# First mixer: four of the modulation parts beside the scan, keys and queries instead of beside the attention and the output projection

## The chip, the cores and the metric

The kernel runs on one core of one Trainium2 chip. The metric is the device time of one execution in microseconds (us), lower is better. Three runs of the kernel before took 1707.82 to 1708.36 us, with a median of 1708.34 us.

## What is computed

The reference is a backbone of two layers over 256 context tokens and 256 latent tokens, 1024 channels wide. Each layer runs three mixers on one shared input projection (a state-space scan, S5; multi-head latent attention; a Hyena long convolution), projects their normed outputs back, and then sends every token through a mixture of 32 experts. What the change moves is the modulation: each layer has six vectors of 1024 channels, worked out from the condition alone, and needed at different places.

```
mod_l = jnp.split((act_l @ ada_w[i] + ada_b[i])[:, None, :], 6, axis=-1)
hl = _modulate(xl, norm1_g[i], mod_l[0], mod_l[1])
...
xl = xl + mod_l[2] * (_merge_groups(s5_l, mla_l, hy_l, mix_norm_g[i]) @ w_out[i])
fl = _modulate(xl, norm2_g[i], mod_l[3], mod_l[4]).reshape(bsz * n, d)
...
xl = xl + mod_l[5] * y[:bsz * n].reshape(bsz, n, d)
```

Parts 0 and 1 are needed first of all, part 2 at the output projection, parts 3 and 4 at the router, part 5 after the experts. `act_l` depends on the condition and on nothing that the layers compute, so any part can be worked out at any time before its use.

## The kernel before, in words

Layer by layer there is a mixer and then the experts. Tokens lie along the free dimension (512 columns, 256 of them context), channels along the partitions in eight blocks of 128. All larger tiles in SBUF are pages of 128 x 1024 fp32 out of one pool of 44 (`NPAGE`), for loaded weights as well as for intermediate results. Loads of weights go through SP's queue, 512 KB each, in the order of the program; a load is issued when a page comes free for it.

One modulation part is `ada_part(i, part)`: eight loads of 512 KB, for each two fp32 matmuls of a 32-column stationary with 512 columns (each stands as two instructions in the trace, so 32 in a part, line 166), an eviction of the PSUM bank (line 121: on ScalarE for even parts, on VectorE for odd ones), four transposes (line 175), two reductions and an addition on VectorE (lines 178 and 179), and for parts 1 and 4 one more VectorE operation (line 183). It yields after four loads, after eight, and at its end.

The order of the work is written with `weave`, which takes one step of each of its generators in turn until all of them are at their end. From that program order a planner with a modelled timeline makes the order of each engine's queue; it may let an instruction that is ready go ahead of an earlier one that is not. The order is fixed when the kernel is built.

The first mixer goes through these stages (times from the profile):

- up to 76 us: parts 0 and 1, and the first input projections;
- first weave, 76 to 113 us: rotation and drive matrices of the scan on VectorE, the chunks, the rope keys and the query latents (projections, line 788), the last of the Hyena spectrum;
- scan weave, 113 to 161 us: the scan on VectorE, the key norm, the Hyena inputs (line 788);
- third weave, 161 to 212 us: the readout matrices of the scan (VectorE, and line 618 on TensorE), the query norm, the keys and values (lines 1016 and 1028), the queries (line 1049);
- attention weave, 212 to 348 us: `attention` (line 1091 and 1097 the scores, 1123 and 1131 the transposed probabilities, 1143 the values), `hyena_end`, `s5_end`, and `ada_rest` with five modulation parts and the start of the router (lines 665, 672 and 681). In program order a head's scores come before the transposes of the head two before it. Scores, values and the statistics of a norm share three PSUM banks;
- from 348 us: the output projection (line 1373), the router, and from 434 us the experts, whose weights are streamed to the end of the layer.

Of the kernel before, what the change touches and what calls it, by code (L numbers as in the profile page):

```python
# [55 lines left out]
def weave(*gens):  # L56

    gens = [g if isinstance(g, tuple) else (g, 1) for g in gens]
    while gens:
        left = []  # L60
        for g, n in gens:
            for _ in range(n):
                if next(g, gens) is gens:
                    break
            else:
                left.append((g, n))
        gens = left


def build(tc, A, dbg=None):  # L70
# [676 lines left out]
    def mixer(i, acc):  # L747
        pl = plan[0] = PLAN[i]
# [78 lines left out]
        def s5_scan():  # L827

            T, rho = V["rot"], V["rho"]
            Sc = V["Sc"] = [page(), page()]  # L830
            for g8 in range(2):
                stage[0] = "S5s"
                gc = slice(g8 * 512, (g8 + 1) * 512)
                Dr = page()
                D_ = [Dr[:, 0:512], Dr[:, 512:1024]]
                for ri in range(2):
                    b = bank(side=True)
                    for gg in range(8):
                        gq, g = gg // 4, gg % 4
                        nc.tensor.matmul(b[:, gg * 64:gg * 64 + 64], V["T"][ri][g8 * 2 + gq][:, g * 128:(g + 1) * 128],  # L840
                                         Ug(g8 * 8 + gg), start=True, stop=True)
                    bv = b.rearrange("p (g c) -> p g c", g=8)
                    dv = D_[ri].rearrange("p (g c) -> p g c", g=8)
                    nc.gpsimd.memset(dv[:, :, 0:1], 0.0)
                    act(dv[0:64, :, 1:64], bv[0:64, :, 0:63], AF.Copy)
                    act(dv[64:128, :, 1:33], bv[64:128, :, 31::-1], AF.Copy)
                    act(dv[64:128, :, 33:64], bv[64:128, :, 63:32:-1], AF.Copy)
                yield
                stage[0] = "S5s"
                tr, ti = T[0][:, gc], T[1][:, gc]  # L850
                Gp, x = page(), page()
                G = [Gp[:, 0:512], Gp[:, 512:1024]]
                X = [x[:, 0:512], x[:, 512:1024]]
                nc.vector.tensor_mul(X[0], D_[1], ti)
                nc.vector.tensor_mul(G[0], D_[0], tr)
                nc.vector.tensor_mul(G[1], D_[1], tr)
                nc.vector.tensor_mul(X[1], D_[0], ti)
                nc.vector.tensor_add(G[0], G[0], X[0])
                nc.vector.tensor_sub(G[1], G[1], X[1])
                for ri in range(2):  # L860
                    nc.vector.tensor_tensor_scan(D_[ri], rho[:, gc], G[ri], 0.0, OP.mult, OP.add)
                yield
                stage[0] = "S5s"
                nc.vector.tensor_mul(X[0], D_[1], ti)
                nc.vector.tensor_mul(G[0], D_[0], tr)
                nc.vector.tensor_mul(X[1], D_[0], ti)
                nc.vector.tensor_mul(G[1], D_[1], tr)
                for ri, op in ((0, OP.subtract), (1, OP.add)):
                    dv = Sc[ri][:, gc].rearrange("p (g s c) -> p g s c", g=8, s=2)
                    gv = G[ri].rearrange("p (g s c) -> p g s c", g=8, s=2)  # L870
                    xv = X[ri].rearrange("p (g s c) -> p g s c", g=8, s=2)
                    nc.vector.tensor_tensor(dv[0:64, :, s0:], gv[0:64, :, s0:], xv[0:64, :, s0:], op=op)
                    nc.vector.tensor_tensor(dv[64:128, :, s0:], gv[64:128, :, s0:, ::-1], xv[64:128, :, s0:, ::-1], op=op)
                yield
# [86 lines left out]
        def hyena_inputs():  # L961

            half = halves(nq)
            hz = V["hz"] = []
            for m in range(6):
                stage[0] = "PROJ"
                b = project(7 + m, cq0)
                o = half()
                w_ = [chp[:, CP_SW + 6 * j + m:CP_SW + 6 * j + m + 1] for j in range(3)]
                act(o, b, AF.Identity, scale=w_[1], bias=chp[:, CP_SB + m:CP_SB + m + 1])  # L970
                bv = b.rearrange("p (s t) -> p s t", t=NS)
                ov = o.rearrange("p (s t) -> p s t", t=NS)
                nc.vector.scalar_tensor_tensor(ov[:, :, 1:], bv[:, :, :NS - 1], w_[0], ov[:, :, 1:], op0=OP.mult, op1=OP.add)
                nc.vector.scalar_tensor_tensor(ov[:, :, :NS - 1], bv[:, :, 1:], w_[2], ov[:, :, :NS - 1], op0=OP.mult, op1=OP.add)  # L974
                hz.append(o)
                yield
# [17 lines left out]
        def kv_norm():  # L994
            stage[0] = "QKV"
            V["kvn"] = normed(V["kv"], CP_KVG, rstd_of(V["kv"], 256))
            yield

        def q_norm():
            stage[0] = "QKV"  # L1000
            V["cqn"] = normed(V["cq"], CP_QG, rstd_of(V["cq"], 384, nq))
            yield

        def keys_values():
            stage[0] = "QKV"
            kvn = V["kvn"]
            ukv = [weights(1 + k) for k in range(2)]
            half = halves()
            kc, vt = V["kc"], V["v"] = [], []
            yield  # L1010
            for m in range(4):
                stage[0] = "QKV"
                b = bank(side=pl["kvs"] and m % 2)
                for k in range(2):
                    for n, (a_, x_) in enumerate(three(ukv[k], kvn[k])):
                        nc.tensor.matmul(b, a_[:, m * 128:(m + 1) * 128], x_, start=(k == 0 and n == 0), stop=(k == 1 and n == 2))
                for j in range(2):
                    t = half()
                    nc.scalar.copy(t[0:64], b[64 * j:64 * j + 64])
                    nc.scalar.copy(t[64:96], V["kr"])  # L1020
                    kc.append(t[0:96])
                yield
            for t in range(4):
                stage[0] = "QKV"
                b = bank(side=pl["kvs"] and t % 2)
                for k in range(2):
                    for n, (x_, a_) in enumerate(three(kvn[k], ukv[k])):
                        nc.tensor.matmul(b, x_[:, t * 128:(t + 1) * 128], a_[:, 512:1024],
                                         start=(k == 0 and n == 0), stop=(k == 1 and n == 2))
                o = half()  # L1030
                nc.scalar.copy(o, b)
                vt.append(o)
                yield
# [244 lines left out]
        def chain(*gens):  # L1278
            for g in gens:
                yield from g  # L1280

        rstd1 = None
        if i == 0:
# [14 lines left out]
            spectrum = V["spectrum"]()  # L1298
# [10 lines left out]
            first_projections(rstd1)  # L1309
            ahead(1)  # L1310
        first = dict(r=V["rotation"], d=V["drive"] if i == 0 else lambda: iter(()), c=lambda: s5_chunks(V["u"]), a=attention_inputs)
        weave(*(first[c]() for c in pl["first"]), spectrum if i == 0 else iter(()))
        ro = V["readout"]() if i == 0 else iter(())
        n, mid = pl["ro"], pl["mid"]
        tail = iter(())
        if mid in (0, 5):
            weave(s5_scan(), chain(kv_norm(), hyena_inputs()))
            weave((ro, n), chain(q_norm(), keys_values()))
        elif mid in (1, 6):
            weave(s5_scan(), chain(kv_norm(), hyena_inputs()))  # L1320
            weave((ro, n), chain(q_norm(), keys_values(), queries()))
        elif mid in (2, 7):
            weave((chain(s5_scan(), ro), n), chain(kv_norm(), hyena_inputs(), q_norm(), keys_values()))
        elif mid in (3, 8):
            weave((chain(s5_scan(), ro), n), chain(kv_norm(), q_norm(), keys_values(), hyena_inputs()))
        elif mid in (4, 9):
            weave(s5_scan(), (ro, n), chain(kv_norm(), hyena_inputs()))
            weave(q_norm(), keys_values())
        if mid in (0, 2, 3, 4):
            weave(queries())  # L1330
        elif mid > 4 and mid != 6:
            tail = queries()
        parts = [(i, 2), (i, 3), (i, 4)] + ([(1, 1), (1, 0)] if i == 0 else []) + ([(i, 5)] if pl["late"] else [])
        Y = []

        def merged(tl, n, o_, acc=None):
# [6 lines left out]
        router = Router(i)  # L1343

        def ada_rest():
            for p in parts:
                yield from ada_part(*p)
                if p == (i, 4):
                    router.start()
                    yield  # L1350
# [726 lines left out]
```

## Time and profile before

| what | value |
|---|---|
| median of three runs | 1708.34 us |
| the profiled execution | 1709.9 us |
| its span in the profile | 1708.1 us |
| TensorE busy | 1533.8 us, 90% of the span |
| VectorE busy | 888.6 us, 52% |
| ScalarE busy | 482.4 us, 28% |
| mean granted TensorE clock | 0.953 |

The span runs from the first instruction to the last; 1.8 us of the profiled execution lie outside it. Busy time of TensorE counts a matmul from its start to its modelled end, overlaps once. PEclk is the share of the full clock that TensorE was granted: 1.00 is 2.4 GHz and 0.50 is 1.2 GHz, and a value between them is a mean over the two.

### The profile page before, as it was taken

What the parts mean: (1) busy time and instruction counts of PE and PEld (TensorE: products, weight loads), DVE (VectorE), ACT (ScalarE), POOL (GpSimd) and SP (SyncE); (2) the same over time, 40 slices, a digit from 0 to 9 for tenths busy, and PEclk for the clock granted to TensorE, in tenths of its full rate; (3) what the DMA queues carried; (4) which work ended last, traced back from release to release, by engine and by line L of the source; (5) the groups of instructions that cost most, each with busy time, mean ns of one, the idle gap of its engine ahead of it and who ended that gap; (6) DMA issues with size and microseconds to landing.
All of it is one profiled execution on the core that took longest, in us unless ns stands there. A gap on an engine that the chain in (4) does not pass through costs nothing. (4 is left out here: it accounts for less than half of the span.)

```text
span 1708.1 us, 22533 instructions
## 1 busy us (share of the span) xinstructions
PE 1533.8 (90%) x8073; PEld 788.0 (46%) x8073; DVE 888.6 (52%) x2176; ACT 482.4 (28%) x931; POOL 94.7 (6%) x154
## 2 busy tenths in 40 slices
PE   5888889998999999999899597899799999999995
PEld 1676744476433333344233387547534444333322
DVE  6769565545244546864643758455524434333333
ACT  3343544342111121112122534444311111111112
POOL 0000212003000000002000000010100000000000
PEclk9998899998999999999999698998899999999998
DMA  9111244559999999999999112577799999999994
GB/s 343 64 38 62 79 181 162 218 198 351 374 392 407 409 409 409 409 408 372 373 402 409 61 62 99 205 264 267 293 359 409 409 409 409 409 409 409 409 409 184
DMA packets 143300, 510.04 MB, mean 299 GB/s; under 512 B 17995, under 2 KB 18573, under 8 KB 142929
## 3 DMA queue, kind: packets, MB, share of 16 engines
q1 hardware_dynamic: 138736, 495.21, 75.0%
q0 software_dynamic: 4160, 12.82, 2.2%
q8 instruction: 66, 1.08, 0.3%
q10 hardware_dynamic: 288, 0.52, 0.1%
q14 instruction: 50, 0.40, 0.1%
HBM read 504.85 MB, written 3.64 MB: 298 GB/s over the span
## 5 line engine op out<-in xcount | busy, mean ns | idle before, releaser
L1582 PE MATMUL MOEp<-MOEpg,MOEpg 128*64 128x512 f32 x956 | 227.4, 603 | 13.1 <-DMA MOEpg<-in_w 11.9
L1582 PE MATMUL MOEp<-MOEpg,ROUTpg 128*64 128x512 f32 x960 | 220.5, 603 | 8.2 <-DMA MOEpg<-in_w 7.9
L1718 DVE SCALAR_TENSOR_TENSOR MOEpg<-MOEpY,MOEwt,MOEpg 64x512 fp32r<-64x512 f32 x128 | 96.0, 750 | 241.5 <-ACT MOEpg L118 241.4
L1606 PE MATMUL MOEpY<-MOEpg,MOEhT 128*64 128x512 f32 x960 | 219.4, 599 | 1.8 <-DVE MOEhT L1598 1.8
L1620 DVE SCALAR_TENSOR_TENSOR zxT<-MOEpC,zmod,zxT 128x256 f32<-128x256 f32 x385 | 168.2, 479 | 8.2 <-PE MOEpC L1698 2.1
L118 ACT ACTIVATE MOEpg<-MOEpY,MOEwt 64x512 fp32r<-64x512 f32 x128 | 87.3, 682 | 276.3 <-PE MOEpY L1606 212.2
L1588 DVE TENSOR_TENSOR MOEh<-MOEh,MOEp 128x256 f32<-128x256 f32 x65 | 27.3, 420 | 241.9 <-ACT MOEh L118 241.9
L118 ACT ACTIVATE MOEh<-MOEp 128x256 f32<-128x256 f32 x65 | 24.9, 383 | 399.7 <-PE MOEp L1582 399.7
L1688 PE MATMUL MOEpC<-MOEGT,MOEpg 128*128 128x512 f32 (+1 forms) x496 | 130.0, 364 | 6.7 <-DVE zxT L1620 6.0
L1582 PEld LDWEIGHTS MOEp<-MOEpg,ROUTpg 128*64 128x64 f32 x960 | 64.2, 137 | 149.4 <-issue 103.7
L1582 PEld LDWEIGHTS MOEp<-MOEpg,MOEpg 128*64 128x64 f32 x956 | 59.4, 136 | 159.3 <-DMA MOEpg<-in_w 90.5
L1606 PEld LDWEIGHTS MOEpY<-MOEpg,MOEhT 128*64 128x64 f32 x960 | 63.5, 136 | 120.6 <-issue 93.8
L1688 PEld LDWEIGHTS MOEpC<-MOEGT,MOEpg 128*128 128x128 f32 x496 | 75.2, 189 | 61.7 <-issue 26.8
L166 PE MATMUL ADAb<-ADApg,zcact 128*32 128x512 f32 x384 | 76.1, 614 | 12.8 <-DMA ADApg<-in_adaw 12.8
L788 PE MATMUL PROJb<-INPpg,PROJpg 128*128 128x512 f32 (+1 forms) x384 | 73.8, 356 | 6.4 <-DVE PROJpg L974 5.7
L788 PEld LDWEIGHTS PROJb<-INPpg,PROJpg 128*128 128x128 f32 x384 | 63.5, 206 | 15.9 <-ACT PROJpg L118 6.7
L118 ACT ACT_TABLE_LOAD x35 | 44.9, 1283 | 15.7 <-DVE ATTst L1102 5.7
L1657 PE MATMUL MOEpG<-MOEpg,ROUTpg 128*128 128x256 f32 x240 | 44.7, 310 | 1.1 <-DVE MOEpg L1493 1.1
L1657 PEld LDWEIGHTS MOEpG<-MOEpg,ROUTpg 128*128 128x128 f32 x240 | 33.0, 194 | 24.2 <-issue 15.8
L1091 PE MATMUL ATTb<-QKVpg,QKVpg 96*128 96x512 f32 x64 | 35.4, 654 | 7.3 <-ACT ATTpg L118 7.3
L1373 PE MATMUL OUTb<-OUTpg,ATTpg 128*128 128x512 f32 (+1 forms) x192 | 41.3, 380 | 0.0
L1373 PEld LDWEIGHTS OUTb<-OUTpg,ATTpg 128*128 128x128 f32 x192 | 34.9, 214 | 5.3 <-DVE ATTpg L230 0.2
(541 smaller groups left out, 2115.2 us busy)
## 6 DMA issues: line engine op xcount, KB each, us to landing
MOEpg<-in_w SPq DMA_DIRECT2D x719, 512.0 KB
ADApg<-in_adaw SPq DMA_DIRECT2D x96, 512.0 KB
ROUTpg<-in_w SPq DMA_DIRECT2D x61, 512.0 KB
PROJpg<-in_win SPq DMA_DIRECT2D x16, 512.0 KB
ATTpg<-in_wout SPq DMA_DIRECT2D x8, 512.0 KB
OUTpg<-in_wout SPq DMA_DIRECT2D x8, 512.0 KB
QKVpg<-in_uq SPq DMA_DIRECT2D x5, 512.0 KB
MOEpg<-in_win SPq DMA_DIRECT2D x5, 512.0 KB
```

The costliest lines, as they stand in the source:

```text
L118: nc.scalar.activation(out, in_, f, **kw)
L166: nc.tensor.matmul(b[q:q + 32, :], cact[:, k, :], w[:, h * 512:(h + 1) * 512], start=(k < 2), stop=(k >= KD - 2), tile_position=(0, q))
L788: nc.tensor.matmul(b, a_[:, c], b_[k][:, c0:], start=(first and n == 0), stop=(last and n == 2))
L1091: nc.tensor.matmul(b, qc[h][:, nq - NS + qt * 128:nq - NS + (qt + 1) * 128], kc[h], start=True, stop=True)
L1373: nc.tensor.matmul(b, a_[:, c], y_, start=(n == 0 and j == 0), stop=(n == KD - 1 and j == 2))
L1582: nc.tensor.matmul(b[64 * h:64 * h + 64, :], X[:, k, :], w[:, h * 512:(h + 1) * 512], start=(k == 0), stop=(k == KD - 1), tile_position=(0 ...
L1588: nc.vector.tensor_mul(h_, h_, b[:, 256:512])
L1606: nc.tensor.matmul(b[64 * h:64 * h + 64, :], hT[:, k % 2, (k // 2) * 64:(k // 2) * 64 + 64], w[:, h * 512:(h + 1) * 512], start=(k == 0), ...
L1620: nc.vector.scalar_tensor_tensor(xT[:, k, seg(s)], b[:, s * NS - c0:(s + 1) * NS - c0], mod[:, 40 + k, s:s + 1], xT[:, k, seg(s)], op0=OP. ...
L1657: nc.tensor.matmul(b[:, kk * 256:(kk + 1) * 256], hs[t][:, k * 128:(k + 1) * 128], G[:, t].rearrange("p e c -> p (e c)"), start=(t == 0 an ...
L1688: nc.tensor.matmul(b, Y_[p][j][rows, k * 128:(k + 1) * 128], GT_[p][rows], start=(j == 0), stop=(j == 1))
L1718: nc.vector.scalar_tensor_tensor(Y[1][rows_of, h * 512:(h + 1) * 512], b[rows], wt[rows], yh.bitcast(F32), op0=OP.mult, op1=OP.subtract)
```

## The change

Of the five parts in `ada_rest` four move. Parts (0, 2) and (0, 3) become a generator `between`, which joins the first weave and also stands in the two weaves after it; a weave runs its generators to their end, so the first one takes both parts whole. Parts (0, 4) and (1, 1) join the third weave. Part (1, 0) stays beside the attention. The start of the router, which needs parts 3 and 4, came after part (0, 4) in `ada_rest` and is now its first step. The second layer's list of parts is written out and stays what it was.

```
+        between = chain(*(ada_part(*p) for p in (((0, 2), (0, 3)) if i == 0 else ())))
-        weave(*(first[c]() for c in pl["first"]), spectrum if i == 0 else iter(()))
+        weave(*(first[c]() for c in pl["first"]), spectrum if i == 0 else iter(()), between)
...
         elif mid in (1, 6):
-            weave(s5_scan(), chain(kv_norm(), hyena_inputs()))
-            weave((ro, n), chain(q_norm(), keys_values(), queries()))
+            weave(s5_scan(), chain(kv_norm(), hyena_inputs()), between)
+            weave((ro, n), chain(q_norm(), keys_values(), queries()), chain(between, ada_part(0, 4), ada_part(1, 1)))
...
-        parts = [(i, 2), (i, 3), (i, 4)] + ([(1, 1), (1, 0)] if i == 0 else []) + ([(i, 5)] if pl["late"] else [])
+        parts = [(1, 0)] if i == 0 else [(1, 2), (1, 3), (1, 4)]
...
         def ada_rest():
+            if (i, 4) not in parts:
+                router.start()
+                yield
             for p in parts:
                 yield from ada_part(*p)
                 if p == (i, 4):
```

## Rows read from the trace of the kernel before

**Rows 1.** The page: TensorE's share, and GB/s in 40 slices.
```profile
PE 1533.8 (90%) x8073; PEld 788.0 (46%) x8073; DVE 888.6 (52%) x2176; ACT 482.4 (28%) x931; POOL 94.7 (6%) x154
...
GB/s 343 64 38 62 79 181 162 218 198 351 374 392 407 409 409 409 409 408 372 373 402 409 61 62 99 205 264 267 293 359 409 409 409 409 409 409 409 409 409 184
```

**Rows 2.** Stretches: length, busy us of PE, PEld, DVE, ACT, POOL; PEclk, DMA.
```profile
46.80:76.60 29.80, 27.28 (x129) 21.98 (x129) 23.05 (x77) 9.65 (x21) 0.00 (x0) 0.89 0.14 45
76.60:113.50 36.90, 31.81 (x139) 24.47 (x138) 28.38 (x63) 14.40 (x24) 0.28 (x3) 0.92 0.10 36
113.50:161.00 47.50, 44.22 (x230) 37.88 (x229) 36.42 (x52) 19.05 (x32) 0.15 (x2) 0.96 0.23 77
161.00:186.40 25.40, 16.54 (x57) 12.60 (x55) 22.75 (x38) 11.88 (x19) 1.97 (x4) 0.72 0.01 2
186.40:211.70 25.30, 25.17 (x342) 21.43 (x341) 6.76 (x17) 10.44 (x20) 10.73 (x21) 0.94 0.45 116
211.70:301.00 89.30, 81.60 (x439) 41.54 (x438) 53.33 (x105) 42.36 (x88) 17.50 (x16) 0.96 0.50 179
301.00:348.00 47.00, 42.21 (x269) 21.26 (x267) 25.15 (x62) 19.59 (x45) 0.00 (x0) 1.00 0.61 226
```

**Rows 3.** Waits of TensorE, 46 to 213 us: us in total, times, longest.
```profile
PE QKVb L201 <- DVE QKVpg L193: 4.4, 1, 4.4
PE S5bb L459 <- DVE S5apg L440: 3.5, 2, 3.3
...
PE QKVb L1049 <- ACT QKVpg L1019: 3.2, 1, 3.2
```

**Rows 4.** Groups on TensorE, 213 to 348 us: modulation parts and router's start.
```profile
L166 PE MATMUL ADAb<-ADApg,zcact 128*32 128x512 f32 x160 | 32.1, 603 | 0.0
...
L175 PE MATMUL ADAb<-zident,ADApg 128*128 128x128 f32 x20 | 3.1, 276 | 0.8 <-ACT ADApg L121 0.8
L681 PE MATMUL ROUTb<-zident,zmod 128*128 128x128 f32 x16 | 2.3, 282 | 0.2 <-ACT ROUTpg L121 0.2
...
L665 PE MATMUL ROUTb<-ROUTpg,zmod 128*2 128x36 f32 x16 | 0.7, 197 | 0.0
L672 PE MATMUL ROUTb<-ROUTpg,zident 2*128 2x36 f32 x4 | 0.6, 279 | 0.5 <-DVE ROUTpg L666 0.5
```

**Rows 5.** A part's small VectorE work, 211 to 348 us.
```profile
L178 DVE TENSOR_REDUCE zmod<-ADAb x10: 165/165/175, 252.6 to 341.2; 128x8 f32<-128x16 f32 x10
...
L121 DVE COPY ADApg<-ADAb x2: 692/692/692, 283.3 to 328.0; 128x512 f32<-128x512 f32 x2
```

**Rows 6.** SP's queue: loads of query weights, and SP's longest wait.
```profile
156.28 30.15 SPq L114 DMA_DIRECT2D QKVpg<-in_uq  x3
...
SPq L114 <- DVE S5cpg L600: 29.0, 1, 29.0
```

**Rows 7.** PE and ACT in order: last head, values, modulation matmuls.
```profile
322.94 1.12 PE L1091 MATMUL ATTb<-QKVpg,QKVpg 96*128 96x512 f32 x2 [0.80 <-ACT ATTpg L118]
323.99 1.05 PE L166 MATMUL ADAb<-ADApg,zcact 128*32 128x512 f32 x4
...
333.52 2.80 PE L1143 MATMUL ATTb<-ATTpg,QKVpg 128*64 128x256 f32 x22
...
336.84 2.78 PE L166 MATMUL ADAb<-ADApg,zcact 128*32 128x512 f32 x24
...
329.43 0.69 ACT L118 ACTIVATE ATTpg<-ATTb,ATTst 128x512 f32<-128x512 f32 x1 [4.00 <-DVE ATTst L1102]
...
331.22 0.48 ACT L118 ACTIVATE ATTpg<-ATTb,ATTst 128x256 f32<-128x256 f32 x1
```

**Rows 8.** Short stretches: what TensorE did and which clock it was granted.
```profile
170.00:175.00 5.00, 4.43 (x14) 3.72 (x15) 2.88 (x6) 2.09 (x5) 0.37 (x1) 0.50 0.00 0
...
225.00:230.00 5.00, 4.17 (x34) 2.89 (x34) 2.56 (x5) 0.98 (x3) 0.00 (x0) 1.00 0.00 0
...
350.00:355.00 5.00, 3.47 (x11) 2.90 (x12) 3.44 (x6) 4.99 (x7) 0.00 (x0) 0.50 0.72 288
```

## The prediction, made before the run

> **What bounds the kernel now.** I read the page first: TensorE is busy for 90% of the span, VectorE for 52%, and DMA moves 372 to 409 GB/s only while the experts stream their weights; before that it has room [rows 1]. So what counts in the first mixer is TensorE's time: its idle time, and the time in which it runs at half clock. The stretches come next [rows 2]. From 76.6 to 113.5 us TensorE is idle for 36.9 - 31.8 = 5.1 us, at a mean clock of 0.92. From 161.0 to 186.4 it is idle for 25.4 - 16.5 = 8.9 us at 0.72, while VectorE is busy for 22.75 of 25.4 us: VectorE sets the pace there. From 186.4 to 211.7 TensorE has no gap (25.17 of 25.30). In the attention weave, 211.7 to 348.0, it is busy for 123.8 of 136.3 us, so that weave is close to its work. Third, the waits: the early gaps are one or two long waits each, 3.5 us of the drive transposes for VectorE, 4.4 us of the query norm for VectorE, 3.2 us of the queries for ScalarE [rows 3]. These are single holes in a chain; work that depends on nothing can lie in them. Last, SP's queue: its loads come when pages come free, and one load of a query weight waited 29.0 us for its page [rows 6].
>
> **The price of one part.** The five parts beside the attention took 32.1 us of TensorE in line 166 and 3.1 us in line 175 [rows 4], 6.4 + 0.6 = 7.0 us each. It can be less or more: 24 of a part's 32 instructions in a row took 2.78 us, which makes 3.7 + 0.6 = 4.3 us with all pages at hand; four alone, as after the arrival of one page, took 1.05 us, which makes 8.4 + 0.6 = 9.0 us [rows 7]. I take 7.0, since the pages of the moved parts come one by one too. Four parts are 28.2 us (17 to 36).
>
> **What the early stages gain in length.** `between` is run to its end by the first weave, so two parts lie there, two in the third weave, none in the scan weave.
>
> First weave: 14.1 us come in. The room is 5.1 us of idle time and what half clock costs, 31.8 x 0.08 = 2.5 us, since steady work would keep the clock up: 7.6 us. The rest, 6.5 us, pushes back what follows, because the drive products and the key norm behind it feed the scan on VectorE.
>
> Third weave: 14.1 us come in. The room up to 186.4 us is 8.9 us idle and 16.5 x 0.28 = 4.6 us of half clock, 13.5 us. So 0.6 us are over; I take half of the clock's room as not won, 2.3 us more. VectorE, which is full here, gets two parts' small work: four reductions at 0.165 us, one copy at 0.69 us [rows 5], and four tiny operations that I price like a reduction: 2.0 us. Together 4.9 us. After 186.4 us nothing could be hidden.
>
> The loads move with them: 32 of 512 KB on SP, at the full 409 GB/s 1.28 us each, 41 us over 110 us in which DMA is busy for 1 to 23% [rows 2]. They cost no time as transfers; behind them in SP's order wait the weights of the projections, which is the page question below. Two evictions go to ScalarE, busy for less than half of each stretch. Nothing goes to POOL. Early stages: +11.4 us; bounds +2 (parts at 4.3 us lie in the holes, only VectorE's 2.0 us remain) and +30 (28.2 us beside no hole, and VectorE).
>
> **What the attention weave loses.** Up to 301 us three parts go, 21.1 us, one part (1, 0) comes, 7.0 us, and the router's start comes, 0.7 + 0.6 + 2.3 = 3.6 us [rows 4]: 10.5 us less on TensorE. Scores wait on maxima, exponentials and three PSUM banks, so a part of the freed time becomes waiting; I take a third: -7.0 us (0 to -10.5).
>
> From 301 to 348 us two parts and the router's start go, and 42.2 - 14.1 - 3.6 = 24.5 us of work remain. Now the chain of a head shows. The last head's scores began at 322.94, its first exponential ended at 330.12 and its last at 331.70 [rows 7]. Less the 1.05 us of modulation in between, a bank is back after 6.1 us and the head is through after 7.7 us. Three heads are left at 301 us, with the values of one pair between them in the same banks (2.80 us [rows 7]; with the eviction I take 3.4): 6.1 + 3.4 + 6.1 + 7.7 = 23.3 us. From 331.70 to 348.0 there are 16.3 us, of which modulation is 2.78 us and two fours at 1.05 us, 4.9 us; 11.4 remain. The tail takes 34.7 instead of 47.0 us: -12.3 us; bounds -22 (bound by 24.5 us of TensorE alone) and 0 (the clock, below).
>
> Attention weave: -19.3 us. Sum: +11.4 - 19.3 = -7.9 us. What follows (output projection, router, experts, second layer) keeps its work and its order; the experts' loads start as the output projection frees pages, so they start earlier by the same time, and the shift goes through to the end. The profiled execution took 1709.9 us, so 1702.0; the median of the runs lies 1.6 us below it: **1700 us**.
>
> **The rivals.**
> *The first weave pays in full (other side).* The order of the queues is fixed when the kernel is built. If the two parts run a page at a time, ahead of the drive transposes, and the 3.5 us hole stays where it was, the first weave grows by 18.0 us. With 4.9 and -19.3 that is +3.6: 1712. It decides from a growth of 14.4 us on. For it: the transposes waited for VectorE, and the parts do not quicken VectorE. Against: idle time of TensorE just before them is what a ready part fills.
>
> *The clock falls in the tail.* With 24.5 us of work in 34.7 TensorE is busy for 71% of the tail. In 350 to 355 us it was busy for 69% and was granted 0.50, that is 1.2 GHz; in 225 to 230 us it was busy for 83% and kept 1.00, 2.4 GHz [rows 8]. If all of the tail ran at half clock, 24.5 us would become 49, and its saving is gone: +11.4 - 7.0 = +4.4, 1713; with half of it at half clock 36.8 us, a saving of some 9 us and 1703. The Trainium skill, "TensorE: Matmul & The Clock Gate", section "HAM oscillation — how this bites in real kernels", says that matmuls fed in short bursts between waits fall back to half clock and start each burst there; by that rule the thinned tail loses what was taken out of it. The trace agrees in one place and not in the other, so I keep it as a rival. The same mechanism helps early: 170 to 175 us ran at 0.50 [rows 8].
>
> *The pages.* Three loads of query weights took 30.15 us to be issued, the last after a wait of 29.0 us for a page [rows 6], some 10 us a load. 18 pages of two parts now come ahead of the last. If a part's pages are not back in time and it slips by one such step, the queries start 10 us later: +21.4 - 19.3 = +2.1, 1710. Against: a moved part gives its pages back as soon as TensorE has used them, and in the third weave TensorE is waiting. The Trainium skill, "Perfetto Trace Analysis", section "Optimization Strategy", says that gaps that return all through a stretch can mean that SBUF has no room for the next tile; here the waits of SP agree, those of TensorE name VectorE and ScalarE [rows 3].
>
> *Waits take the place of the work.* If the heads' chain sets the weave up to 301 us already (0 instead of -7.0) and the tail gives only 10, the sum is about +1: 1709, no change.
>
> *More than forecast.* Parts at 4.3 us in the holes: early +2, attention -19.3: -17, 1691.
>
> **How the numbers follow.** Within 0.2%, 3.4 us, no change can be told. Chances: forecast 0.48 (its own range 1693 to 1707, from early +7 to +15 and attention -16 to -22), more 0.09, first weave 0.15, clock 0.12, pages 0.09, waits 0.07. Faster: nearly all of the first two, a third of the clock, a little of the rest, 0.60. Slower: most of the first weave, a third each of the clock and the pages, 0.20. The same: 0.20. The range of 8 in 10 takes in the rivals above and part of the larger gain: 1688 to 1714.
>
> **What will show it.** Right: in the first weave TensorE's wait of 3.5 us for line 440 is gone, the wait of 4.4 us for line 193 is mostly gone, and the clock between 161 and 190 us is over 0.9; the first scores come some 11 us later, at 223 us; the output projection starts near 344 us instead of 352. Wrong: those waits stand beside the parts; or the tail shows 0.5 in its clock; or the queries wait for a load; or the attention weave is no shorter than 130 us.

## The result and the profile after

The change makes the kernel slower: 1722.4 us against 1708.4 us, a ratio of 1.0086 with a 95% interval of 1.0068 to 1.0103. The forecast was 1700 with a range up to 1714. Now and then an execution falls into a slower state and takes far longer (2240.3 us, one of six of e3 below); all medians here are without such runs. The profiled execution took 1722.2 us (1709.9 before), its span is 1720.0 us (1708.1), the mean granted clock 0.949 (0.953).

Five instants are the same piece of work in every kernel here and cut the first mixer into weaves: the first chunk transposes of the scan (line 806, where the first projections end), the first drive products (840), the first keys (1016), the first scores (1091) and the first output projection (1373; 1377 in the changed kernel, where lines from 1347 on stand four later).

| us | 806 | 840 | 1016 | 1091 | 1373 | first weave | scan | third weave | attention |
|---|---|---|---|---|---|---|---|---|---|
| before | 74.4 | 113.5 | 161.0 | 211.7 | 352.4 | 39.1 | 47.5 | 50.7 | 140.7 |
| after | 74.2 | 127.3 | 174.5 | 235.8 | 361.9 | 53.1 | 47.2 | 61.3 | 126.1 |

The first weave grows by 14.0 us, the third by 10.6, the attention shrinks by 14.6. The output projection starts 9.5 us later, the first expert 9.2 us (443.3 against 434.1). From there to the end it is 1276.7 us against 1274.0; in the 18 runs below that stretch took 1271 to 1280 us, whatever was edited ahead of it, so its 2.7 us lie within that spread and are not put down to the change.

The stretches of the changed kernel (length; busy us of PE, PEld, DVE, ACT, POOL; PEclk; DMA share; GB/s), to be held against [rows 2]:

```profile
76.60:127.30 50.70, 44.53 (x208) 26.25 (x208) 29.56 (x69) 14.71 (x24) 0.28 (x3) 0.93 0.46 156
127.30:174.50 47.20, 43.92 (x231) 37.66 (x230) 36.42 (x51) 19.35 (x33) 0.15 (x2) 0.96 0.21 71
174.50:199.90 25.40, 19.39 (x91) 12.17 (x89) 22.71 (x37) 9.52 (x16) 1.11 (x3) 0.80 0.68 262
199.90:235.80 35.90, 33.24 (x378) 25.84 (x379) 8.46 (x28) 13.25 (x24) 11.52 (x23) 0.95 0.42 130
235.80:322.20 86.40, 76.06 (x410) 45.51 (x409) 52.08 (x107) 42.39 (x90) 17.32 (x16) 0.92 0.18 64
322.20:361.90 39.70, 30.37 (x167) 18.43 (x165) 21.06 (x45) 20.21 (x45) 0.00 (x0) 0.92 0.44 162
```

The last stretch runs to the output projection, 4.4 us further than the last one of [rows 2]. Cut alike, the kernel before has:

```profile
301.00:352.40 51.40, 44.16 (x281) 23.13 (x280) 26.76 (x64) 23.73 (x51) 0.00 (x0) 0.97 0.64 243
```

Read length less PE's busy time. In the first weave TensorE is idle for 6.2 us, where it was 5.1 before; in the third for 6.0 + 2.7 = 8.7, where it was 8.9 + 0.1. In sum, the idle time that was to take the parts is all still there, and TensorE's busy time stands on top of it: 12.7 and 10.9 us more. Two of the waits of [rows 3] have hardly changed; the third, 3.2 us of the queries, is gone, and one of 2.7 us for the readout (line 600) has come:

```profile
PE QKVb L201 <- DVE QKVpg L193: 4.5, 1, 4.5
PE S5bb L459 <- DVE S5apg L440: 3.7, 2, 2.5
PE S5cb L618 <- DVE S5cpg L600: 2.7, 1, 2.7
```

Why the wait for line 440 did not go is seen on VectorE and ScalarE, in order of time (start, us, instruction, idle time before it and what ended it):

```profile
105.65 0.59 ACT L121 COPY ADApg<-ADAb 128x512 f32<-128x512 f32 x1 [9.92 <-PE ADAb L166]
106.13 1.06 ACT L118 ACTIVATE PROJpg<-PROJpg 128x1024 fp32r<-128x1024 f32 x1
...
107.22 1.23 DVE L230 TENSOR_TENSOR PROJpg<-PROJpg,PROJpg 128x1024 fp32r<-128x1024 f32 x1 [5.54 <-ACT PROJpg L118]
110.92 0.26 DVE L178 TENSOR_REDUCE zmod<-ADAb 128x8 f32<-128x16 f32 x2 [2.47 <-PE ADAb L175]
...
120.82 0.69 DVE L121 COPY ADApg<-ADAb 128x512 f32<-128x512 f32 x1 [4.61 <-PE ADAb L166]
121.43 0.68 DVE L435 TENSOR_TENSOR PROJpg<-S5apg,S5apg 128x512 f32<-128x512 f32 x1
```

ScalarE stands for 9.9 us at the eviction of part 2, whose last matmuls have not run; behind it in its queue is the split of a weight (line 118), behind that on VectorE the other half of the split (230), and behind that the expansion (435 to 444) for which the drive transposes wait. The weight itself isn't late: its load was issued at 92.5 us, and the one just ahead of it landed 4.5 us after its issue, so by estimate it was there at 97 us, 9 us before its split. Twice more VectorE stands at a part's own small work, 2.5 and 4.6 us, with expansion behind it that needs nothing of the part. Together 12.6 us. The Trainium skill, "Perfetto Trace Analysis", section "Tensor Engine Instruction (MATMUL, LD_WEIGHTS)", says that ScalarE and VectorE take their instructions strictly in order; the trace agrees, line 435 starts at 121.43 us, 0.6 us after the start of the copy that held it.

On TensorE the pages' matmuls of the two parts stand alone or in small groups among the projections:

```profile
87.83 1.05 PE L166 MATMUL ADAb<-ADApg,zcact 128*32 128x512 f32 x4
...
89.40 1.06 PE L166 MATMUL ADAb<-ADApg,zcact 128*32 128x512 f32 x8
...
102.44 1.05 PE L166 MATMUL ADAb<-ADApg,zcact 128*32 128x512 f32 x4
...
104.55 1.05 PE L166 MATMUL ADAb<-ADApg,zcact 128*32 128x512 f32 x4
```

Four instructions of one page take as long as eight of two pages; what that is worth is tried below. The group rows of lines 166 and 175 over the first weave, and of line 166 over the attention, where [rows 4] had 32.1 us for five parts:

```profile
L166 PE MATMUL ADAb<-ADApg,zcact 128*32 128x512 f32 x64 | 12.7, 702 | 0.0
L175 PE MATMUL ADAb<-zident,ADApg 128*128 128x128 f32 x8 | 1.3, 280 | 0.8 <-DVE ADApg L121 0.8
...
L166 PE MATMUL ADAb<-ADApg,zcact 128*32 128x512 f32 x32 | 8.4, 605 | 0.0
```

### The profile page after: what moved, and what is told of

The parts are those of the page before. It is cut to its first block, busy times and chain, and to the rows that moved or that the text cites. A ratio compares the mean times of both kernels' runs of the same rounds, so it can differ in the third digit from the quotient of the medians.

```text
span 1720.0 us, 22536 instructions
## 1 busy us (share of the span) xinstructions
PE 1538.5 (89%) x8073; PEld 790.8 (46%) x8073; DVE 885.3 (51%) x2176; ACT 481.4 (28%) x930; POOL 94.6 (5%) x154
## 3 DMA queue, kind: packets, MB, share of 16 engines
HBM read 504.85 MB, written 3.64 MB: 296 GB/s over the span
## 5 line engine op out<-in xcount | busy, mean ns | idle before, releaser
L788 PEld LDWEIGHTS PROJb<-INPpg,PROJpg 128*128 128x128 f32 x384 | 62.1, 202 | 19.0 <-ACT PROJpg L118 6.6
L1708 POOL TENSOR_TENSOR zxT<-zxT,MOEpg 128x512 f32<-128x512 f32 (+1 forms) x6 | 6.0, 1002 | 538.9 <-ACT MOEpg L118 538.9
```

The costliest lines, as they stand in the source:

```text
L788: nc.tensor.matmul(b, a_[:, c], b_[k][:, c0:], start=(first and n == 0), stop=(last and n == 2))
```

## The experiments

All were timed beside the kernel before, whose median was 1710 to 1711 us on those chips; a ratio is to it, with its 95% interval behind it. The code fences show the edits shortened; `...` marks what is left out. Lengths are the weaves of the table above.

**Halves of the change.** e1 moves only parts (0, 2) and (0, 3); e2 only (0, 4) and (1, 1).

```
e1: weave((ro, n), chain(q_norm(), keys_values(), queries()))
    parts = [(0, 4), (1, 1), (1, 0)] if i == 0 else ...
e2: between = chain(*(ada_part(*p) for p in ()))
    parts = [(0, 2), (0, 3), (1, 0)] if i == 0 else ...      (router.start() after (0, 3))
```

> Only (0, 2) and (0, 3) move, into the first weave; (0, 4), (1, 1) and (1, 0) stay beside the attention. If the two halves of the change are independent (my theory: the cost is waits inside the first weave), the drive products start at 127 us as in the whole change (113.5 before), the first scores at 225 (+13.5 to 14), the attention gives back half of 14.7, that is 7.4: about 1715. If the halves share their cost (the rival: the 32 loads and pages of all four parts crowd each other), the drive products start before 122 us and the time is below 1711.

> Only (0, 4) and (1, 1) move, into the third weave; (0, 2), (0, 3), the router's start and (1, 0) stay beside the attention. Independent halves: drive products at 113.5 as before, third weave longer by 10.7, first scores at 222, attention 7.4 shorter: about 1712. Shared cost: third weave longer by less than 6, and a time at or below 1707.

e1: 1725.9 us (1.0075, 1.0052 to 1.0097); first weave 51.5 (+12.4), third 50.6 (as before), attention 140.1 (-0.6). e2: 1728.6 us (1.0100, 1.0083 to 1.0116); first weave 38.6, third 62.1 (+11.4), attention 146.0 (+5.3). The early costs are independent, each half pays its own. The gain is not: each half was expected to give back 7.4 us beside the attention (1715 and 1712 us in all), and neither gives back anything. In e1 TensorE is busy there for 120.5 us instead of 125.8, at a mean clock of 0.93 instead of 0.97, and idle for 19.6 instead of 14.9; two parts' matmuls are gone, and waiting and a slower clock have taken their place. Why the attention of e2 is even 5.3 us longer, no run explains.

**The finish of a part later.** e3 is e1 with the eviction, transposes, reductions and additions of the two parts put into the scan weave.

```
-        between = chain(*(ada_part(*p) for p in ...))
+        between = chain(*(ada_part(*p, finish=finish) for p in ...))    # stops behind the matmuls
-            weave(s5_scan(), chain(kv_norm(), hyena_inputs()), between)
+            weave(s5_scan(), chain(kv_norm(), hyena_inputs()), chain(*(ada_finish(*f) for f in finish)))
```

> As e1, but in the first weave only the loads and the matmuls of the two parts; their evictions, transposes, reductions and additions come in program order with the scan weave. My theory (evictions and reductions stand in the in-order queues of ScalarE and VectorE ahead of the weight splits and the expansion, and wait there for late modulation matmuls, 12.6 us of VectorE's waits): drive products at 115 to 120 us, time 1706 to 1710. Rival (the projections' weights themselves come later, because 16 modulation pages come ahead of them): drive products still at 124 to 127, time 1713 to 1716. Rival (TensorE has no room for 13 us of matmuls): the same 124 to 127, and then without waits of VectorE.

1724.0 us (1.0082, 1.0063 to 1.0100), slower than either time expected, with the drive products at 121.6, between the two expectations. First weave 46.8: 4.7 us less than in e1, so the stalls at the evictions cost about that. The time is only 1.9 us under e1's: the scan weave, where the finish now is, takes 49.6 (47.3 in e1), though it is as long in e11, e12, e15 and e18, where the finish is not in it. VectorE still waits 9.1 us in one place, for the split of a weight (line 230, here 243). The rest of the growth, 7.7 us, had another cause.

```profile
DVE PROJpg L243 <- ACT PROJpg L118: 9.7, 2, 9.1
```

**No loads.** e4 is the kernel before with two more parts in the first weave that read the resident input; e18 the same in the third weave.

```
+    spare parts: w = xT[:, k, :] in place of load(adaw[i, part, k]); result into mods[1], written again later
e4:  weave(*(first[c]() for c in pl["first"]), spectrum ..., between)
e18: weave((ro, n), chain(q_norm(), keys_values(), queries()), chain(two spare parts))
```

> The kernel before, with two more parts in the first weave that load nothing: their matmuls read the resident input instead of modulation weights, their result goes to a place that is written again later. All five real parts stay beside the attention, so the time shows the growth of the first weave alone. If late loads are at the root of the cost, the growth is what TensorE's work needs beyond its holes, 4 to 7 us: drive products at 118 to 121, time 1712 to 1715. If TensorE's work alone costs it, with or without loads: 12 to 14 us, drive products at 125 to 127, time 1720 to 1722.

> The kernel before, with two more parts in the third weave that load nothing (as e4 for the first weave). All five real parts stay beside the attention. If the idle time of the third weave (9 us up to 186) can take matmuls whose data is there, first scores at 210 to 214 and the time at 1708 to 1712: then it is the loads that come too late for the hole. If TensorE's time is paid in full there, first scores at 218 to 221, 1716 to 1720.

e4: 1710.3 us (0.9993, 0.9982 to 1.0004): no cost at all, first weave 38.3, better than either expectation. Its two parts on TensorE:

```profile
45.77 3.64 PE L166 MATMUL ADAb<-zxT,zcact 128*32 128x512 f32 x32
...
102.77 3.64 PE L166 MATMUL ADAb<-zxT,zcact 128*32 128x512 f32 x32
```

Each part runs in one go, one in the 2.9 us hole before the first projections, one where TensorE waited for line 440, and both together take 7.3 us instead of 12.7. The wait for line 440 falls from 3.5 to 0.8 us, and the granted clock of the first weave rises from 0.92 to 1.00. So holes can be filled, by work that is at hand when they open; but only one of the two parts lay in the first weave, so for two this is not shown. e18: 1716.2 us (1.0033, 1.0019 to 1.0046), first scores at 214.3, third weave 53.1 (+2.4). That is far from 10.6, but the evidence is mixed: one of its parts ran at 46 us, in the same early hole as in e4, and only the other lay in the third weave, at 182; the hole before line 201 was not used (a wait of 5.3 us), and the time grew by more than the first scores moved.

**Loads alone.** e11 is the kernel before with the 16 loads of two more parts in the first weave, each read by one matmul of 8 columns.

```
+                    w = load(A["adaw"][0, p, k])
+                    nc.tensor.matmul(b[0:32, k * 8:k * 8 + 8], cact[:, k, :], w[:, 0:8], start=True, stop=True)
```

> The kernel before, with the 16 loads of two more parts in the first weave, each read by one matmul of 8 columns; no modulation matmuls, no eviction, nothing behind them, all five real parts beside the attention. If the places in the ring and in SP's order cost the first weave, the drive products start at 117 to 125 us and the time is 1712 to 1720. If it is TensorE's work and what waits behind it, they start at 111 to 115: 1707 to 1711.

1712.7 us (1.0008, 0.9997 to 1.0019), first weave 40.1 (+1.0), first scores 213.8. The places in the ring of pages, SP's order and the transfers cost about one us in the first weave, two up to the first scores. Neither the loads alone (e11) nor matmuls without loads (e4) cost the 14.0 us. What is left is the two together: matmuls that run late, as their pages come one by one, with other engines' work held up behind them.

**Other pages, another queue.** The whole change, with the 32 moved loads in two pages of their own (e5 on POOL's queue, e6 on SP's), or in the shared pages on POOL's queue (e7).

```
+        t = own[0].tile([128, 1024], F32, ...)      # e5, e6: a pool of two; e7: t = page()
+        nc.gpsimd.dma_start(t, src)                 # e6: nc.sync
```

> The whole change, but the loads of the four moved parts take two pages of their own, outside the 44, and go through POOL's queue. If the modulation loads cost by standing in the one ring of pages and in SP's order (my theory after e4), the first weave grows by -2 to +3 as without loads, the third by 0 to 5, first scores at 212 to 222 (235.8 in the change), the attention takes 126 as in the change: 1694 to 1706. If the transfers themselves or the later matmuls cost it, first scores stay at 228 to 236 and the time at 1715 to 1722; two pages for 32 loads could also make the parts' matmuls late in the same way.

> As e5, with the loads in SP's queue. If the places in the 44 pages are the cost, as e5 (1694 to 1706). If SP's order is (a load that waits for its page holds up the projections' weights behind it), as the change or worse: 1718 to 1730, and SP waits for line 166.

> The whole change with its 44 shared pages, only that the loads of the four moved parts go through POOL's queue. If SP's order is the cost, like e5: 1694 to 1706. If the places in the ring are the cost, like the change: 1716 to 1724.

All three are slower than the change: 1735.1 (1.0143, 1.0125 to 1.0161), 1732.9 (1.0134, 1.0111 to 1.0156) and 1730.3 us (1.0112, 1.0093 to 1.0130); first weaves of 58.9, 56.3 and 56.2. My theory then, that the ring and SP's order were the cost, fell. With two pages the matmuls come later still, and VectorE stands longer at the eviction; in e5, where line 175 is the modulation matmul:

```profile
130.19 0.69 DVE L121 COPY ADApg<-ADAb 128x512 f32<-128x512 f32 x1 [16.39 <-PE ADAb L175]
```

**A part in one go, or in pairs.** e9 holds a part's matmuls back until its eighth page is there, e10 issues them two pages at a time, both in the whole change. e12 does the pairs in the kernel before and moves nothing. The edit of e10 and e12, shortened; in e9 all eight pages are loaded first and the eighth page's matmuls stand first:

```
-        for k in range(KD):
-            w = load(adaw[i, part, k])
+        for k0 in range(0, KD, 2):
+            pair = [load(adaw[i, part, k]) for k in (k0, k0 + 1)]
+            with ExitStack() as behind:
+                for k in (k0 + 1, k0):                       # the later page first
                     for h in range(2): mm = nc.tensor.matmul(...)
+                        if k > k0 and not h:
+                            behind.enter_context(tc.issue_after(mm.ins))
```

> The whole change; the 32 matmul instructions of a part stand in one go, behind the arrival of its eighth page, instead of four by four as the pages come. The rows show four instructions of one page in 1.05 us, eight of two pages in 1.06 and 32 in 3.64, so a part in one go should take 3.6 us of TensorE instead of 6.2. If that price is what the first weave pays (12.3 us in line 166), it grows by 8 to 10 instead of 13.9, the third by 8 to 9 instead of 10.7: 1712 to 1717. If waits for pages are the cost, the eight pages held together make it worse: 1722 to 1732.

> The whole change; all modulation matmuls are issued two pages at a time, the four instructions of the later page first and those of the earlier one behind them. If a lone page costs as much as two, line 166 falls from 12.3 to 7.5 us in the first weave and likewise elsewhere: first weave +9, first scores at 227 to 231, time 1710 to 1717. If TensorE's price isn't the cost: 1719 to 1725.

> The kernel before, with nothing moved: only its modulation matmuls are issued two pages at a time as in e10. Beside the attention line 166 took 30.3 us of TensorE in 29 groups; in pairs 18 to 20. If a part's price on TensorE is what the attention pays, the output projection starts 5 to 12 us earlier than at 352: 1697 to 1704. If the attention is held by waits and the clock: 1707 to 1711.

e9: 1736.2 us (1.0160, 1.0138 to 1.0182), first weave 58.4: ScalarE waits 16.0 us at one eviction, VectorE 11.6 and 8.0 us at two. e10: 1719.6 us (1.0052, 1.0036 to 1.0068); first weave 55.5, not shorter but 2.4 us longer, with TensorE idle for 9.1 us of it; attention 125.2. As long as the weave is held by stalls at the evictions, cheaper matmuls there gain nothing. e12: **1700.4 us (0.9943, 0.9923 to 0.9963)**, the fastest kernel here, 10.4 us under the kernel before. Its attention takes 135.3 instead of 140.7 us, with line 166 (168 in this kernel) at 20.5 us where [rows 4] has 32.1:

```profile
L168 PE MATMUL ADAb<-ADApg,zcact 128*32 128x512 f32 x160 | 20.5, 602 | 0.0
```

The whole attention weave of the kernel before and of e12, with the same work on TensorE (x718):

```profile
211.70:352.40 140.70, 125.76 (x718) 64.67 (x717) 80.09 (x169) 66.08 (x139) 17.50 (x16) 0.97 0.55 202
213.40:348.70 135.30, 119.17 (x718) 66.50 (x717) 78.84 (x168) 64.25 (x137) 17.48 (x16) 0.94 0.56 207
```

The output projection starts 3.7 us earlier, less than the 5 to 12 us expected: the stretch up to the first projections is 1.8 us longer, the scan weave 2.1, the third weave 1.7 shorter (49.0). From the first expert to the end it is 1271.1 us, 2.9 less than before and the shortest of all. The pairs are at work there too, in the second layer's parts (17.0 us of line 168 where line 166 took 23.1), but e10, e16 and e17 have the same 17.0 us and take 1274.6 to 1277.6. So about half of the gain is seen beside the attention; the rest I can't tie to a place.

**Work without loads beside the attention.** e8 is the whole change, and at the old places of the four parts four that load nothing, with the router's start behind the third of them.

> The whole change, and beside the attention four parts without loads (matmuls on the resident input, result overwritten later) at the places that the four real parts had. If the attention became 14.7 us shorter because TensorE's work left it, it goes back to 138 to 142: 1734 to 1738. If the loads and their pages were what it lost, it stays at 126 to 131: 1721 to 1727. Where the clock stays up through the extra work, a value between them.

1737.7 us (1.0165, 1.0147 to 1.0183). The attention takes 138.6, 12.5 more than in the change. Only three of the four parts lay in it, so that is 4.2 us a part; the 32 matmuls of the first ran from 223.3 us on, ahead of the first scores at 239.0, and the third weave took 67.9 us instead of 61.3. So the gain of the change beside the attention was the work that left it, not its loads.

**The weights first.** e13 is e3 and e15 the whole change, with the loads of the next four projection weights ahead of the modulation loads; e14 is e2, with the query weights ahead of them; e15 does that too. e16 adds to e15 the pairs and the late finish. e17 is e16 without the third weave's half: (0, 4) and (1, 1) stay beside the attention.

```
+        if i == 0:
+            mixer_weights[i].fetch(4)       # ahead of the first weave: e13, e15, e16, e17
...
+            mixer_weights[i].fetch(5)       # ahead of the third weave: e14, e15, e16
```

> As e3 (finish late), and the loads of the next four projection weights come ahead of the modulation loads in SP's order and in the ring. My theory now: with the modulation loads in front, the fourth of these weights comes late, its split stands behind a projection's eviction in ScalarE's queue, and VectorE waits 9.1 us for it in front of the expansion. Then that wait goes, and the drive products start at 112 to 116 us (121.6 in e3, 113.5 before); time 1713 to 1718. If TensorE's 10.7 us in line 166 are the cost, they still start at 120 to 122 and the time stays at 1721 to 1726.

> As e2 (third half only), and the loads of the keys', values' and query weights come ahead of the modulation loads. If the third weave pays for the last query weight, whose load came behind 12 modulation loads, first scores at 211 to 215 (221.5 in e2, 211.7 before), time 1718 to 1723. If it pays for TensorE's work and for the slower readout chain: 219 to 222, 1726 to 1730.

> The whole change with both sets of weights loaded ahead of the modulation. Late weights as the cause: the first weave grows by 5 to 9 (the two waits at the parts' evictions stay), the third by 1 to 4, first scores at 218 to 225, the attention stays at 126: 1704 to 1712. TensorE's time as the cause: first scores at 232 to 236, 1719 to 1724.

> e15, and besides all modulation matmuls in pairs of pages (as e10) and the finish of the first two parts in the scan weave (as e3). If the reasons are right, first weave +0 to 4, third +1 to 4, attention 124 to 126: 1692 to 1702, faster than both kernels. If not, 1710 or more.

> Only (0, 2) and (0, 3) move, into the first weave, with all that mended it in e16: weights loaded first, pairs of pages, finish in the scan weave. (0, 4), (1, 1) and (1, 0) stay beside the attention, in pairs. First weave +1 to 3, third weave as before. If the two parts give back what four gave from 135.3 (e12) to 125.2 (e10), 5 us: 1696 to 1700, at or under e12 (1700.4). If two parts give nothing back, as in e1: 1702 to 1706.

| | us | ratio, 95% interval | first weave | scan | third weave | attention |
|---|---|---|---|---|---|---|
| e13 | 1721.4 | 1.0061 (1.0042 to 1.0081) | 46.4 | 49.7 | 49.7 | 141.5 |
| e14 | 1727.8 | 1.0102 (1.0084 to 1.0121) | 39.1 | 47.4 | 59.7 | 144.7 |
| e15 | 1722.2 | 1.0068 (1.0051 to 1.0084) | 49.1 | 49.7 | 60.5 | 129.5 |
| e16 | 1707.9 | 0.9983 (0.9967 to 0.9999) | 40.7 | 51.4 | 63.0 | 125.5 |
| e17 | 1710.8 | 0.9992 (0.9978 to 1.0006) | 40.6 | 51.4 | 50.9 | 134.2 |

The lengths of e16 and e17 are from executions of 1716.8 and 1716.7 us, 9 and 6 us above the medians of these kernels. e15 came out as expected for TensorE's time as the cause (1719 to 1724 us, first scores at 232.4), not for late weights; e16 and e17 missed what was expected of them (1692 to 1702 us; 1696 to 1700, or 1702 to 1706).

e13 tells most. The wait of 9.1 us for the split is gone, as I expected, and the weave is no shorter than in e3; its pages come more often alone, and line 166 takes 13.5 us instead of 11.2. The stretch from line 806 to 840, first of e13, then of e16:

```profile
74.60:121.00 46.40, 45.30 (x234) 25.74 (x233) 32.57 (x69) 14.54 (x25) 0.28 (x3) 1.00 0.42 148
```

```profile
76.00:116.70 40.70, 39.60 (x234) 25.36 (x233) 32.40 (x69) 14.40 (x25) 0.28 (x3) 1.00 0.48 166
```

In both TensorE has no more than 1.1 us of idle time, at full clock: the hole is filled, and what remains of the growth is TensorE's own work, 7.3 us with lone pages, 1.6 us in pairs. e14 refutes the query weights as the cost of the third weave: 9.0 us of growth remain. Its third weave:

```profile
161.20:220.90 59.70, 50.72 (x470) 36.50 (x468) 31.23 (x63) 24.35 (x43) 12.63 (x24) 0.91 0.49 167
```

Its longest wait of TensorE in that weave, the one of [rows 3]:

```profile
PE QKVb L201 <- DVE QKVpg L193: 5.0, 1, 5.0
```

TensorE is busy for 50.7 us where it was 41.7, and idle for 9.0 as before: whatever comes in is paid in full. The pairs don't help there: in e16 the third weave is the longest of these, 63.0 us, which no run explains. Mended in all these ways the placement (e16) is 0.2% under the kernel before, and its half (e17) equal to it, while the pairs without any move (e12) gain 0.6%.

## Why the prediction was wrong

**The step that failed: what the early stages gain in length,** forecast +11.4, measured +24.1 (first scores 235.8 against 211.7). It makes 12.7 of the 22 us by which the time was missed; the attention weave makes 4.7 and the stretch behind the first expert, with no cause shown, 2.7.

*First weave, forecast +6.5, measured +14.0.* The balance of TensorE (14.1 us in, 7.6 us of room) was right by itself: 12.7 + 1.3 us came in, and with the stalls removed (e13) the weave grows by 7.3 us, TensorE idle for 1.1. What was not priced are, by that difference, the other 6.7 us: the part's eviction, reductions and copy stand in the in-order queues of ScalarE and VectorE ahead of the splits and the expansion. The prediction counted them as work that fits beside other work and asked of no instruction what would wait behind it. With the expansion late, the 3.5 us hole moved along with it instead of being filled. e3 (finish later: 4.7 us less), e5, e6 and e9 (later matmuls: longer stalls, 17 to 20 us of growth) and e4 (no late matmul: no growth, with one part in the weave) show this from both sides.

*Third weave, forecast +4.9, measured +10.6.* Here the balance itself was wrong: 13.5 us of room were counted, and in sum none of the idle time was used. The forecast counted all of the work ahead of the readout products (line 618), behind which, as it said, nothing could be hidden. Those products start 27.9 us after the first keys in the change (25.4 before), with TensorE busy for 19.4 us (16.5). From there to the first scores it is 33.4 us (25.3), with TensorE busy for 33.2 (25.2): 8.1 of the 10.6 us came in where it had no gap. 28 of the 64 modulation instructions ran there, and the first query projections (line 1049), which had run at 183.6 us ahead of the readout products, came behind them. The hole before line 201 ended at 180.6 us with nothing in it:

```profile
171.27 1.96 SPq L114 DMA_DIRECT2D ADApg<-in_adaw  x4
180.55 3.57 PE L201 MATMUL QKVb<-zones,QKVpg 128*128 128x2 f32 x16 [4.55 <-DVE QKVpg L193]
191.18 2.77 PE L166 MATMUL ADAb<-ADApg,zcact 128*32 128x512 f32 x20
```

Late query weights are excluded (e14). Late modulation loads are not enough: from 171 to 180 us DMA moved 195, 238 and 403 GB/s in three stretches, by estimate 2.5 MB or more than four loads, and 419 GB/s or 2.1 MB more to 185 us; yet the first matmul ran at 191.2. And e18, with no loads, did not use that hole either. So for the pages that were there it is the order of TensorE's queue that left it empty; why the planner built it so stays open. The shift of the first half moved the hole too, and the prediction took it as standing still.

**The attention weave,** forecast -19.3, measured -14.6. The tail behind the scores of head 5 came out in size: 39.7 us where it had been 51.5, -11.8 against -12.3. A little of that is luck: of the two fours of modulation counted behind 331.70 us one had run at 329.96, and without it the sum gives -11.2. Up to there -2.8 instead of -7.0. TensorE's busy time fell by 5.5 us (81.6 to 76.1), for 9.7 us of work that went (22.3 us of modulation out; 9.0 of part (1, 0) and 3.6 of the router's start in), its idle time rose by 2.6. The clock is a part of it: 0.92 where [rows 2] has 0.96. Three stretches of 5 us in a row, of the changed kernel:

```profile
285.00:290.00 5.00, 5.00 (x13) 2.24 (x12) 0.69 (x1) 3.78 (x8) 1.55 (x2) 1.00 0.00 0
290.00:295.00 5.00, 3.84 (x24) 2.74 (x22) 3.71 (x9) 4.71 (x10) 0.00 (x0) 0.93 0.00 0
295.00:300.00 5.00, 5.00 (x21) 3.91 (x22) 2.92 (x8) 1.08 (x3) 2.49 (x2) 0.50 0.01 2
```

TensorE idled for 1.2 us, between 291 and 293; the clock fell in 294 to 295 us, with TensorE busy again, and for the next five us it worked at 1.2 GHz without a gap. The rival on the clock was thus real, in the first part of the weave and in the tail, which came out as forecast all the same (0.92 against 0.97 in the rows cut alike). The mean over the weave fell from 0.97 to 0.92, and to 0.88 in e16. By estimate that is half clock for 16% of 126 us instead of 6% of 141, some 12 us more, which can cost 6 us at most. The Trainium skill, "TensorE: Matmul & The Clock Gate", section "HAM oscillation — how this bites in real kernels", on which that rival drew, says that matmuls fed in short bursts between waits fall back to half clock. The fall of the mean goes that way; what brought the fall at 294 us is not shown, nor how much of the time the clock took alone.

**The price of one part,** 7.0 us, held in the first weave (14.0 us for two) and was low elsewhere (15.6 us for two in the third weave, 9.0 for part (1, 0) beside the attention). But it is a price of the order, not of the work. The prediction had both rows in hand, 24 in 2.78 and four in 1.05 us [rows 7], and put the difference down to pages that come one by one, as a given. e12 shows that it can be changed where the parts already were.

**The rivals.** The first weave in full had the right place, the right sign and nearly its size (14.0 of 18.0, deciding from 14.4); added to it was a third weave that also paid in full, which no rival had. The pages were not it (e11, e14; two parts have 16 pages, not 18). A chance of 0.15 on the first was too little: its argument against, that a ready part fills idle time, says nothing of a part that is not ready, or that the queue's order puts elsewhere.

## What to carry to other kernels

Idle time of an engine takes moved work only if its data is there when the hole opens and the order of the queue puts it there; ask for each moved step when its loads land, and what stands behind its eviction in the queues of the engines that evict. Price a step by what its instructions cost in the order in which they will run, in one go and alone, before moving it: here the cheaper order at the old place was worth more than the move. And what a full stage gives back when work leaves it is less than that work, since waits and a lower clock take a share; two halves that gain nothing each can gain 14 us together.

## What was not expected of the hardware

Four modulation instructions of one page take 1.05 us, eight of two pages 1.06, 32 of eight pages 3.64 (e9, at full clock). In the code the two halves of a page go to two column groups of 32 (`tile_position=(0, q)`, `q = 32 * (2 * (k % 2) + h)`), so an even and an odd page use four different ones. The Trainium skill, "TensorEngine Tiling (Array Packing)", section "Key Properties", says that such tiles work independently and can execute matmuls in parallel; the rows agree, with the condition that the instructions of an even and an odd page stand next to each other in TensorE's queue. With other work between them each page takes its 1.05 us; in pairs (e12) the five parts beside the attention took 20.5 us instead of 32.1.
